# A hybrid decoder layer on one core: residual additions and the split of a late operand go in front of older ready work

## The chip, the core and the metric

The kernel runs on one NeuronCore of a Trainium2 chip. It uses five engines, each with its own instruction stream: TensorE (PE, matrix products, with a separate stream of weight loads, PEld), VectorE (DVE), ScalarE (ACT), GpSimd (POOL) and SyncE (SP, which here only issues transfers). The engines meet through semaphores, and each works through its own stream in order. The metric is the time of one execution on the device in microseconds (us): the median over repeated runs. One more execution was recorded by the hardware profiler; its trace is what is read below.

## What is computed

One decoder layer over 1024 tokens of width 1024: RWKV-7 time mixing and a sparse attention side by side, merged by gates, then a dense feed-forward block and a last normalisation. Cut to what the change touches:

```python
merged = g_a * (y_a @ w_o_rwkv) + g_b * (y_b @ w_o_att)
h = h + merged @ w_out
z = rmsnorm(h, norm2_g) @ w_ffn_in
z_gate, z_up = jnp.split(z, 2, axis=-1)
h = h + (jax.nn.silu(z_gate) * z_up) @ w_ffn_out
return rmsnorm(h, normf_g)
```

`y_a` comes from the RWKV recurrence over 64 x 64 states, `y_b` from the attention, in which each token attends to at most 256 keys that an indexer picked. The feed-forward width is 2816.

## The kernel before

**Tiles.** Activations lie with channels on the 128 partitions and tokens along the free dimension, in two halves of 512 tokens; the kernel calls them half 0 and half 1. Half 0 is the first half. A matrix of 1024 channels is eight slices of 128 x 512. Products are made to float32 accuracy from parts: `split` turns an operand into a rounded part on ACT (line 117) and a remainder on DVE (line 118), and a product is hi x hi, hi x lo and lo x hi (lines 143, 144 and 148, or 161 in `mm3_last`, or 1545, 1546 and 1548 in `joint`), 24 matmuls of 128 x 512 for 8 input slices. A weight slice comes by DMA into `wst` (three buffers, line 124) and is split into `whi` and `wlo` (two buffers each), at high priority. A product lands in one of three PSUM banks named `acc` or five named `mix`. Scratch `tmp` is a ring of four 128 x 512 buffers.

**Feed-forward.** The 22 slices of the feed-forward width go in three groups of 8, 8 and 6 (`GROUPS`). For the first two groups, `ffn_in` makes the gated slices and `ffn_out` multiplies them with the group's part of `w_ffn_out`: for each of eight output slices d it loads the running residual `d_h` from HBM into a `tmp` (line 1382), makes the product in an `acc` bank, adds the two on DVE (line 1388, the residual addition) and stores the result back (line 1392, on SP). With three banks, the product of slice d+3 cannot begin until the addition of slice d has read its bank. The last group of both halves is made together in `joint`, with the seven products of a Strassen-Winograd scheme: it first normalises half 1 (line 1575), loads half 0's operand again from `d_z` (line 1584, issued on POOL) and makes the combinations T1 and T2 (lines 1592, 1604 and 1610), and later T3 and T4 (lines 1592, 1633 and 1634), each split on ACT and DVE. `s_12271`, `s_12296`, `s_12554` and `s_12571` in the order below are T1 to T4, `s_12329` is B22.

**What runs beside what.** `fill` is a queue of generators; `pump` takes matmuls from it between the steps of the latency-bound stages. So half 0's `merge`, `ffn_in` and `ffn_out` of its first group stand between the steps of half 1's RWKV recurrence and its attention, and the output of half 0's middle group between half 1's `merge` and the start of `joint`. In the recurrence, each step goes S (line 885), products (850), `rhs` (860, four additions on DVE), products (869), `UV` (872 on ACT), products (881) and S again. Beside its last steps the selection of attention keys ends (lines 1053 to 1060), with scratch from the same `tmp` ring.

**The operand of half 0.** `normalise` makes half 0's feed-forward operand anew from `h` while the first slices of `ffn_in` run: four slices `za`, then four slices `zb` by way of `ts`, which are split last: the late split.

**What sets the order.** On PE the order is that of the program. On the other engines a scheduler chooses at build time among the instructions that it takes to be ready, and by default the older in program order goes first; what stands under `tc.high_priority()` goes in front. At run time every engine follows the order so chosen.

Of the kernel before, what the change touches and what calls it, by code (L numbers as in the profile page):

```python
# [19 lines left out]
ALU = mybir.AluOpType  # L20
# [30 lines left out]
def block_kernel(ctx: ExitStack, tc: tile.TileContext, ins: dict, outT: bass.AP, outR: bass.AP, stop=None, dbg=None):  # L51
    nc = tc.nc
    V, A, G, T, SY = nc.vector, nc.scalar, nc.gpsimd, nc.tensor, nc.sync
# [59 lines left out]
    def tmp():  # L113
        return tp.tile([128, HT], F32, tag="tmp", name="tmp")

    def split(hi, lo, x):
        A.activation(hi, x, AF.Copy)  # L117
        V.tensor_tensor(lo, x, hi.bitcast(F32), op=ALU.subtract)  # L118
# [8 lines left out]
    def weights(src, nk=8, rush=True, st=None, pool=None):  # L127
        with tc.high_priority() if rush else nullcontext():
            if st is None:
                st = raw_weights(src, nk)  # L130
            hi, lo = ((pool or wp).tile([128, nk, 128], F32R, tag=tag, name=tag, bufs=8 if pool else None)
                      for tag in ("whi", "wlo"))
            split(hi, lo, st)
        return hi, lo
# [3 lines left out]
    def mm3(ps, w, act, nk=8, wk=0, ak=0, tok=None):  # L138
        whi, wlo = w
        ahi, alo = act  # L140
        tok = slice(0, HT) if tok is None else tok
        for k in range(nk):
            T.matmul(ps, whi[:, wk + k, :], ahi[:, ak + k, tok], start=k == 0, stop=False)  # L143
            T.matmul(ps, whi[:, wk + k, :], alo[:, ak + k, tok], start=False, stop=False)  # L144
            if k % 2:
                yield 4
        for k in range(nk):
            T.matmul(ps, wlo[:, wk + k, :], ahi[:, ak + k, tok], start=False, stop=k == nk - 1)  # L148
            if k % 4 == 3 or k == nk - 1:
                yield k % 4 + 1  # L150

    def mm3_last(pss, ws, act, nk, tok=slice(0, HT), within=False):

        ahi, alo = act

        def terms(i, ks, js=range(3)):
            ps, (whi, wlo) = pss[i], ws[i]
            for j in js:
                w, a = ((whi, ahi), (wlo, ahi), (whi, alo))[j]
                for k in ks:  # L160
                    T.matmul(ps, w[:, k, :], a[:, k, tok], start=k == 0 and j == 0, stop=k == nk - 1 and j == 2)  # L161
                yield len(ks)

        n = len(pss) - within
        for i in range(n):
            yield from terms(i, range(nk - 1))
        if within:
            yield from terms(n, range(nk - 1), range(2))
        for i in range(n):
            yield from terms(i, range(nk - 1, nk))  # L170
        if within:
            yield from terms(n, range(nk - 1), (2,))
            yield from terms(n, range(nk - 1, nk))
# [17 lines left out]
    def but_last(gen):  # L191

        opened_tile[0] = True
        prev = next(gen)
        for n in gen:
            yield prev
            prev = n
        opened_tile[0] = False
        return prev
# [1091 lines left out]
    def parts(t):  # L1291
        return [t[:, k, :] for k in range(4)], [t[:, 4 + k, :] for k in range(4)]

    def normalise(zp, sq, row):

        h = sq.h

        def one(k, out):
            V.scalar_tensor_tensor(out, h[:, k, :], par[:, P_N2 + k:P_N2 + k + 1], row, op0=ALU.mult, op1=ALU.mult)
            SY.dma_start(d_z[k], out)  # L1300

        low, ts = zp.tile([128, 8, HT], F32R, tag="s2", name="za"), []
        for k in range(4):
            one(k, h[:, k, :])
            split(low[:, k, :], low[:, 4 + k, :], h[:, k, :])
        for k in range(4):
            ts.append(tmp() if k < 3 else tp.tile([128, HT], F32, tag="sacc", name="zt", bufs=2))
            one(4 + k, ts[k])
        high = zp.tile([128, 8, HT], F32R, tag="s0", name="zb")
        for k in range(4):  # L1310
            split(high[:, k, :], high[:, 4 + k, :], ts[k])
        return [Planes(*(a + b)) for a, b in zip(parts(low), parts(high))]

    def ffn_in(zp, tags, zs, gi, box):
# [4 lines left out]
        for j in range(gn):  # L1319
# [15 lines left out]
            if j < early:  # L1335
                x = tmp()
                V.tensor_tensor(x, pg, row, op=ALU.mult)
                A.activation(t, x, AF.Tanh, scale=0.5)
                V.scalar_tensor_tensor(t, t, 1.0, x, op0=ALU.add, op1=ALU.mult)
                V.scalar_tensor_tensor(x, pu, 0.5, row, op0=ALU.mult, op1=ALU.mult)  # L1340
                V.tensor_tensor(t, t, x, op=ALU.mult)
                if j == 0:
                    z = normalise(zp, sq, row)
                    opened_tile[0] = False
                    yield 4
                else:
                    zs[0] = z
            else:
                A.activation(t, pg, AF.Tanh, scale=0.5)
                V.scalar_tensor_tensor(t, t, 1.0, pg, op0=ALU.add, op1=ALU.mult)  # L1350
                V.scalar_tensor_tensor(t, pu, 0.5, t, op0=ALU.mult, op1=ALU.mult)
# [10 lines left out]
    def ffn_out(half, zp, f, gi, sqs=None):  # L1362
        gn = GROUPS[gi][1]
        final = sqs is not None
        if final:
            h = zp.tile([128, 8, HT], F32, tag="s2", name="h")
            sqs.append(Rms(h))
            for d in range(8):
                G.dma_start(h[:, d, :], d_h[half][d])

        def w(d):
            return weights(ins["w_fo1"][d] if final else ins["w_fo0"][gi, d], gn)

        bank = mix if final else acc
        pss = [bank() for _ in range(1 if final else 2)]
        last = yield from but_last(mm3_last(pss, [w(d) for d in range(len(pss))], f, gn, within=half == 1))
        for d in range(8):
            if final:
                t = h[:, d, :]
            else:  # L1380
                t = tmp()
                SY.dma_start(t, d_h[half][d])
            if d < len(pss):
                ps = pss[d]
            else:
                ps = bank()
                last = yield from but_last(mm3(ps, w(d), f, nk=gn))
            V.tensor_tensor(t, t, ps, op=ALU.add)  # L1388
            if final:
                sqs[0].add(d)  # L1390
            else:
                SY.dma_start(d_h[half][d], t)
            if d >= len(pss) - 1:
                yield last
# [99 lines left out]
    def ffn(half, zp, zs, tags):  # L1494

        for gi in range(JOINT):
            f = []
            yield from ffn_in(zp, tags, zs, gi, f)
            yield from ffn_out(half, zp, f[0], gi)
# [281 lines left out]
    credit[0] = 0  # L1781
    pump_whole(144 - 8)
    run_over(ffn_out(0, zp0, fj, JOINT, sq0))
    pump_whole(48)
    run_over(norm_out(0, sq0[0]))
# [90 lines left out]
```

## Time and profile before

| | us |
|---|---|
| median of three runs | 1756.36 (1756.19 to 1757.58) |
| profiled execution, its own time | 1753.59 |
| its span in the trace | 1751.7 |
| mean granted clock of TensorE | 0.988 of full speed |
| DVE busy in the span | 1127.6 (64%) |
| ACT busy | 869.6 (50%) |
| POOL busy | 133.8 (8%) |
| the 32 residual additions of line 1388 on `tmp` | 0.68 each, first at 924.2, last at 1709.0 |
| products of the first group's output, half 0 | from 904.74 to the next stage's first product at 977.18 |

A row of the order of time reads: start, duration, engine, line, operation, output<-inputs, shapes, count; at its end, in brackets, how long the engine sat idle before it and what released it. Starts are in us from the start of the span. Matmuls are pipelined, so a row's duration can reach over the next start; differences of starts are what counts.

### The profile page before, as it was taken

The page shows a single profiled execution, that of the slowest core. Times are in us where ns is not written, and L with a number is a line of the kernel's source. Part 1 is how long each engine was busy: PE and PEld are TensorE (multiplying, and loading weights), DVE is VectorE, ACT ScalarE, POOL GpSimd, SP SyncE. Part 2 cuts the span into 40 slices and gives each one's busy share as a digit, 9 for nine tenths or more (in the row PEclk, how much of TensorE's full clock was granted, in tenths as well). Part 3 has the DMA queues.
Part 4 walks back from the last instruction along what each step waited for, and adds up shares of the span by engine and source line. Part 5 has one row for each costly group of instructions (what it writes and reads, how often), then busy time and mean ns, then how long its engine had stood idle before and what let it go on. Part 6 is the DMA issues. An engine that isn't in the chain of part 4 may idle for free.

```text
span 1751.7 us, 26667 instructions
## 1 busy us (share of the span) xinstructions
PE 1694.3 (97%) x10000; PEld 1395.7 (80%) x10000; DVE 1127.6 (64%) x2206; ACT 869.6 (50%) x1685; POOL 133.8 (8%) x183
## 2 busy tenths in 40 slices
PE   8999999999999999999999999999979999999997
PEld 6888888888878777877787888888857788888887
DVE  6789899866577567858856544466577655433344
ACT  6365998554455788665334365533334333222322
POOL 0000000010022110001000311011000100000001
PEclk9999999999999999999999999999989999999999
DMA  5542334545376436734343764266622633553362
GB/s 209 178 139 87 107 91 141 174 108 160 109 214 169 146 102 197 225 112 137 90 121 100 228 172 127 91 226 203 187 83 90 193 112 108 172 168 102 115 214 80
DMA packets 144448, 253.44 MB, mean 145 GB/s; under 512 B 49680, under 2 KB 71888, under 8 KB 144192
## 3 DMA queue, kind: packets, MB, share of 16 engines
q1 hardware_dynamic: 115760, 161.84, 29.8%
q10 hardware_dynamic: 16128, 48.60, 8.8%
q0 software_dynamic: 12432, 41.30, 8.1%
q8 instruction: 79, 1.29, 0.3%
q14 instruction: 49, 0.40, 0.1%
HBM read 193.45 MB, written 58.25 MB: 144 GB/s over the span
## 4 chain that ended last, share of the span: by engine, by line
PE 41%; issue 6%; DVE 2%; DMA 1%; ACT 1%; POOL 1%; POOLq 0%; DVEq 0%; ACTq 0%
PE acc L148 9%; PE acc L143 9%; PE acc L144 9%; PE acc L161 3%; PE mix L1124 1%; PE mix L1100 1%; PE mix L1114 1%; PE mix L1548 1%; PE mix L1546 1%; PE mix L1545 1%; PE mix L148 1%; PE mix L144 1%; PE mix L143 1%; DMA wst<-in_w_ffn_in 0%; DMA d_h<-tmp 0%
## 5 line engine op out<-in xcount | busy, mean ns | idle before, releaser
L118 DVE TENSOR_TENSOR wlo<-wst,whi 128x1024 fp32r<-128x1024 f32 (+1 forms) x203 | 248.1, 1223 | 246.0 <-ACT whi L117 130.0
L117 ACT ACTIVATE whi<-wst 128x1024 fp32r<-128x1024 f32 (+1 forms) x203 | 212.6, 1049 | 278.4 <-PE acc L144 212.5
L143 PE MATMUL acc<-u1hi,whi 128*128 128x512 f32 x320 | 127.9, 400 | 0.0
L144 PE MATMUL acc<-u1lo,whi 128*128 128x512 f32 x320 | 125.1, 391 | 0.0
L143 PE MATMUL acc<-u0hi,whi 128*128 128x512 f32 (+1 forms) x320 | 122.8, 386 | 0.0
L144 PE MATMUL acc<-u0lo,whi 128*128 128x512 f32 (+1 forms) x320 | 121.3, 382 | 0.0
L143 PE MATMUL acc<-s,whi 128*128 128x512 f32 x256 | 99.8, 390 | 0.0
L144 PE MATMUL acc<-s,whi 128*128 128x512 f32 x256 | 99.6, 389 | 0.0
L143 PE MATMUL acc<-fhi,whi 128*128 128x512 f32 x192 | 76.9, 401 | 12.6 <-DVE tmp L1388 12.6
L148 PE MATMUL acc<-u1hi,wlo 128*128 128x512 f32 x320 | 81.8, 394 | 0.0
L148 PE MATMUL acc<-u0hi,wlo 128*128 128x512 f32 (+1 forms) x320 | 78.6, 384 | 0.0
L144 PE MATMUL acc<-flo,whi 128*128 128x512 f32 x192 | 76.0, 396 | 0.0
L1015 ACT ACTIVATE junkl<-kept,z 128x1024 int8<-128x1024 int16 (+1 forms) x64 | 69.4, 1084 | 4.7 <-DVE kept L984 4.4
L143 PEld LDWEIGHTS acc<-u1hi,whi 128*128 128x128 f32 x320 | 60.1, 188 | 12.6 <-issue 0.9
L1105 ACT ACTIVATE L<-L,mx 128x128 f32<-128x128 f32 (+7 forms) x64 | 49.5, 774 | 41.4 <-DVE mx L1102 40.8
L143 PEld LDWEIGHTS acc<-u0hi,whi 128*128 128x128 f32 x320 | 60.2, 188 | 11.9 <-issue 0.4
L144 PEld LDWEIGHTS acc<-u1lo,whi 128*128 128x128 f32 x320 | 60.2, 188 | 11.3
L144 PEld LDWEIGHTS acc<-u0lo,whi 128*128 128x128 f32 x320 | 60.2, 188 | 11.0
L148 PEld LDWEIGHTS acc<-u1hi,wlo 128*128 128x128 f32 x320 | 58.9, 188 | 12.5 <-issue 0.9
L148 PEld LDWEIGHTS acc<-u0hi,wlo 128*128 128x128 f32 x320 | 58.1, 188 | 11.9 <-issue 0.7
L148 PE MATMUL acc<-s,wlo 128*128 128x512 f32 x256 | 63.2, 389 | 0.0
L148 PEld LDWEIGHTS acc<-s,wlo 128*128 128x128 f32 x256 | 48.0, 188 | 10.0
(476 smaller groups left out, 4080.7 us busy)
## 6 DMA issues: line engine op xcount, KB each, us to landing
wst<-in_w_ffn_in SPq DMA_DIRECT2D x61, 512.0 KB
wst<-in_w_in ACTq DMA_DIRECT2D x36, 512.0 KB
wst<-in_w_in SPq DMA_DIRECT2D x27, 512.0 KB
wst<-in_w_fo SPq DMA_DIRECT2D x25, 512.0 KB
k<-d_k POOLq DMA_DIRECT2D x24, 512.0 KB, 8.0
d_g<-tmp ACTq DMA_DIRECT2D x32, 256.0 KB
wst<-in_w_ffn_in ACTq DMA_DIRECT2D x16, 512.0 KB
tmp<-d_h SPq DMA_DIRECT2D x32, 256.0 KB
```

The source lines that it names most:

```text
L117: A.activation(hi, x, AF.Copy)
L118: V.tensor_tensor(lo, x, hi.bitcast(F32), op=ALU.subtract)
L143: T.matmul(ps, whi[:, wk + k, :], ahi[:, ak + k, tok], start=k == 0, stop=False)
L144: T.matmul(ps, whi[:, wk + k, :], alo[:, ak + k, tok], start=False, stop=False)
L148: T.matmul(ps, wlo[:, wk + k, :], ahi[:, ak + k, tok], start=False, stop=k == nk - 1)
L161: T.matmul(ps, w[:, k, :], a[:, k, tok], start=k == 0 and j == 0, stop=k == nk - 1 and j == 2)
L1015: A.activation(junka[:, :n], y, AF.Sign, bias=z[:, i:i + 1], accum_out=cnt[:, i:i + 1])
L1100: T.matmul(ps[:, :w], q[bi // 2][:, e, bi % 2 * 128:bi % 2 * 128 + 128], k[:, i, e, c:c + w], start=i == 0, stop=i == 1)
L1105: A.activation(L[:, :n], L[:, :n], AF.Exp, scale=-1.0, bias=last, accum_out=sm[:, bi, e:e + 1])
L1114: T.transpose(ps[:, j * 128:(j + 1) * 128], L[:, (c + j) * 128:(c + j + 1) * 128], ident)
L1124: T.matmul(py[64 * e:64 * e + 64, bi * 128:(bi + 1) * 128], v[:, j, 64 * e:64 * e + 64], pts[e][j // 4][:, j % 4, :], start=j == b, stop=j ...
L1545: T.matmul(ps, whi[:, k, :], hi[k], start=opens and k == 0, stop=False, skip_group_check=True)
```

## The change

Two places change. In `normalise`, the four splits of the late slices are put under high priority. In `ffn_out`, the residual addition is put under high priority where it is not the last group's; loads, products, weight splits and the store keep theirs.

```diff
         high = zp.tile([128, 8, HT], F32R, tag="s0", name="zb")
-        for k in range(4):
-            split(high[:, k, :], high[:, 4 + k, :], ts[k])
+        with tc.high_priority():
+            for k in range(4):
+                split(high[:, k, :], high[:, 4 + k, :], ts[k])
         return [Planes(*(a + b)) for a, b in zip(parts(low), parts(high))]
...
-            V.tensor_tensor(t, t, ps, op=ALU.add)
+            with nullcontext() if final else tc.high_priority():
+                V.tensor_tensor(t, t, ps, op=ALU.add)
             if final:
                 sqs[0].add(d)
```

No instruction is added or removed, and PE's stream and POOL's stay as they were. After the change, lines behind 1309 have numbers higher by one and those behind 1387 by two (1388 becomes 1390, 1575 becomes 1577 and so on).

The first place is DVE's stream at the start of `joint`, where the output of half 0's middle group ends. Before, the piece behind the normalisation reads as follows; the addition of the first row is that of d=3, and `wlo` is the weight split of d=6, then of d=7.

```order
L1388 TENSOR_TENSOR tmp<-tmp,acc 128x512
L1575 SCALAR_TENSOR_TENSOR h<-h,par,row 128x512 x2
L1604 TENSOR_TENSOR t_12273<-h,t_12273 128x512
L1604 TENSOR_TENSOR t_12279<-h,t_12279 128x512
L1575 SCALAR_TENSOR_TENSOR h<-h,par,row 128x512
L118 TENSOR_TENSOR wlo<-wst,whi 128x1024
L118 TENSOR_TENSOR s_12271<-t_12273,s_12271 128x512
L118 TENSOR_TENSOR s_12271<-t_12279,s_12271 128x512
L1604 TENSOR_TENSOR t_12285<-h,t_12285 128x512
L1575 SCALAR_TENSOR_TENSOR h<-h,par,row 128x512 x2
L118 TENSOR_TENSOR s_12271<-t_12285,s_12271 128x512
```

Between this piece and the next stand 20 rows more, with the weight splits of d=7 and of the first product of `joint` among them. Then the additions of d=4, 5 and 6 follow, and after another weight split that of d=7:

```order
L1610 TENSOR_TENSOR t_12322<-t_12322,t_12324 128x512
L118 TENSOR_TENSOR s_12329<-h,s_12329 128x512
L1388 TENSOR_TENSOR tmp<-tmp,acc 128x512
L118 TENSOR_TENSOR s_12296<-t_12322,s_12296 128x512
L1388 TENSOR_TENSOR tmp<-tmp,acc 128x512 x2
L1523 TENSOR_TENSOR sr<-wst 128x512
L118 TENSOR_TENSOR sw<-sr,sw 128x512
L1528 TENSOR_TENSOR sr<-sr,wst 128x512
L118 TENSOR_TENSOR wlo<-wst,whi 128x1024
L1388 TENSOR_TENSOR tmp<-tmp,acc 128x512
```

After the change, the same stream from the addition of d=3:

```order
L1390 TENSOR_TENSOR tmp<-tmp,acc 128x512
L1577 SCALAR_TENSOR_TENSOR h<-h,par,row 128x512 x2
L1606 TENSOR_TENSOR t_12273<-h,t_12273 128x512
L1606 TENSOR_TENSOR t_12279<-h,t_12279 128x512
L1577 SCALAR_TENSOR_TENSOR h<-h,par,row 128x512
L1390 TENSOR_TENSOR tmp<-tmp,acc 128x512
L118 TENSOR_TENSOR wlo<-wst,whi 128x1024
L118 TENSOR_TENSOR s_12271<-t_12273,s_12271 128x512
L118 TENSOR_TENSOR s_12271<-t_12279,s_12271 128x512
L1606 TENSOR_TENSOR t_12285<-h,t_12285 128x512
L1577 SCALAR_TENSOR_TENSOR h<-h,par,row 128x512 x3
L1390 TENSOR_TENSOR tmp<-tmp,acc 128x512
```

The addition of d=4 stands ahead of the weight split of d=6, that of d=5 ahead of the weight split of d=7; those of d=6 and d=7 stand in the same way ahead of the next two weight splits.

The second place is DVE's stream in the last steps of half 1's recurrence, where the output of half 0's first group begins. Before, from the `rhs` of one step to the S of the next:

```order
L860 TENSOR_TENSOR rhs<-mix,rhs 64x2x64 x4
L1388 TENSOR_TENSOR tmp<-tmp,acc 128x512
L118 TENSOR_TENSOR wlo<-wst,whi 128x1024 x2
L1388 TENSOR_TENSOR tmp<-tmp,acc 128x512
L884 TENSOR_TENSOR S<-mix,S 128x256
L885 TENSOR_TENSOR S<-S,PC 128x256
L899 TENSOR_TENSOR yb<-mix,yb 128x512
L1056 TENSOR_SCALAR cnt<-cnt 128x1
L901 TENSOR_REDUCE mn<-yb 128x8
```

After the change the same piece:

```order
L860 TENSOR_TENSOR rhs<-mix,rhs 64x2x64 x3
L1390 TENSOR_TENSOR tmp<-tmp,acc 128x512 x2
L118 TENSOR_TENSOR wlo<-wst,whi 128x1024 x2
L860 TENSOR_TENSOR rhs<-mix,rhs 64x2x64
L884 TENSOR_TENSOR S<-mix,S 128x256
L1056 TENSOR_SCALAR cnt<-cnt 128x1
L885 TENSOR_TENSOR S<-S,PC 128x256
L899 TENSOR_TENSOR yb<-mix,yb 128x512
L901 TENSOR_REDUCE mn<-yb 128x8
```

Both additions and, with them, both weight splits now stand ahead of the fourth `rhs` addition. One step later (rows not shown here) the selection's lines 1054 and 1055 move ahead of the four `rhs` additions of that step, and each later addition ahead of the weight split next to it.

The third place is the late split on DVE. The rows are the same before and after; ACT's rows of `zb` are as well.

```order
L1299 SCALAR_TENSOR_TENSOR zt<-h,par,row 128x512
L118 TENSOR_TENSOR wlo<-wst,whi 128x1024
L118 TENSOR_TENSOR zb<-tmp,zb 128x512 x3
L604 TENSOR_SCALAR x_8281<-x_8281 128x1024
L631 TENSOR_SCALAR x_8323<-x_8282,hb 128x256
L606 SCALAR_TENSOR_TENSOR x_8281<-rmask,x_8281 128x256
L118 TENSOR_TENSOR zb<-zt,zb 128x512
```

Nothing moved there.

## The prediction

> **What bounds the kernel now.** I read the page first, then the waits of TensorE (PE), then the order of time around the longest of them.
>
> ```profile
> PE 1694.3 (97%) x10000; PEld 1395.7 (80%) x10000; DVE 1127.6 (64%) x2206; ACT 869.6 (50%) x1685; POOL 133.8 (8%) x183
> ```
>
> TensorE is busy for 1694.3 of 1751.7 us. Its program order is written out by hand, so whatever it waits for delays everything behind. The change can win only out of the 57.4 us in which PE is idle, and out of the stretches after a wait in which its clock is lower.
>
> ```profile
> PE acc L143 <- DVE tmp L1388: 12.6, 1, 12.6
> ...
> PE acc L143 <- ACT zb L117: 3.3, 1, 3.3
> PE mix L869 <- DVE rhs L860: 3.2, 2, 2.6
> ```
>
> This is the view of who waited for whom (total, times, longest). The longest wait of the whole run is a single one: a product that needs an `acc` bank waits for a residual addition (L1388). The second row belongs to the late split (`zb`), the third to the end of the RWKV stage, where the other set of moved additions stands. Those three places are the case.
>
> ```profile
> 1259.36 0.39 PE L143 MATMUL acc<-fhi,whi 128*128 128x512 f32 x1
> ...
> 1262.99 1.98 PE L148 MATMUL acc<-fhi,wlo 128*128 128x512 f32 x8
> ...
> 1282.97 0.77 PE L143 MATMUL acc<-fhi,whi 128*128 128x512 f32 x1 [12.57 <-DVE tmp L1388]
> ...
> 1288.03 1.98 PE L148 MATMUL acc<-fhi,wlo 128*128 128x512 f32 x8
> ```
>
> In the order of time on PE (start, duration), slice d=5 of the middle group starts at 1259.36, so d=4 was finished then and its addition could run. Slice d=7 needs the bank of d=4 and waits 12.57 us. Its first 16 products then take 1288.03 - 1282.97 = 5.06 us, where those of d=5 took 1262.99 - 1259.36 = 3.63: 1.43 us more, at a lowered clock (the granted clock stands third from the end in the rows of stretches below).
>
> ```profile
> 1259.06 0.74 DVE L1575 SCALAR_TENSOR_TENSOR h<-h,par,row 128x512 f32<-128x512 f32 x1
> ...
> 1282.15 0.68 DVE L1388 TENSOR_TENSOR tmp<-tmp,acc 128x512 f32<-128x512 f32 x1
> ```
>
> VectorE (DVE) held that addition back from 1259.80 to 1282.15, behind normalisations, combinations and splits of `joint` that were ready.
>
> **The change, part by part.** No instruction is added or removed.
>
> *The joint start, the main term.* The addition of d=4 now stands right behind the instruction of 1259.06, so it ends near 1260.4. Slice d=7 can begin when d=6 ends, at 1282.97 - 12.57 = 1270.40; the bank is free 10 us before. The wait of 12.57 and the 1.43 at the lowered clock go: 14.0 us on PE.
>
> What is late next? VectorE must do the same work in less time:
>
> ```profile
> 1256.50:1321.10 64.60, 50.14 (x77) 0.92 0.31 101
> 1255.00:1285.00 30.00, 25.65 (x40) 0.84 0.46 143
> 1285.00:1303.00 18.00, 7.18 (x11) 0.98 0.11 42
> 1303.00:1321.00 18.00, 17.27 (x30) 1.00 0.29 87
> ```
>
> These are VectorE's busy times by stretch (stretch, length, busy time, granted clock of PE, share of the DMA engines, GB/s). Between the row factor's arrival (1256.5) and the last split of the fourth combination (T4), it is busy 50.14 of 64.60 us. The room is 14.46 us, most of it in 1285 to 1303, where it waited for PE. Without PE's gap it needs 50.14 us in 64.60 - 14.0 = 50.6. And T4 was already a wait:
>
> ```profile
> 1321.13 0.50 PE L1546 MATMUL mix<-s,sw 128*128 128x512 f32 x1 [0.31 <-DVE s L118]
> ```
>
> So PE gains what VectorE gains: 14.46 less the idle that stays. What stays are waits for others:
>
> ```profile
> 1266.36 0.69 DVE L1604 TENSOR_TENSOR t<-h,t 128x512 f32<-128x512 f32 x1 [1.69 <-DMA t<-d_z]
> ...
> 1278.53 0.69 DVE L1610 TENSOR_TENSOR t<-t,t 128x512 f32<-128x512 f32 x1 [1.20 <-DMA t<-d_z]
> ```
>
> These two make 2.89 us; the loads are issued when a split releases a buffer, and the additions (0.68 each) that now stand among these instructions fill a part. At worst all idle of the first and third stretch stays, 4.35 + 0.73 = 5.08: a gain of 9.4. At best 0.46 stays: 14.0. I take two thirds of the two rows, 1.9, and so **12.5**.
>
> SP issues the store of each addition in order, and in the new order the stores of d=4, 5 and 6 stand between the loads of the next weights, where all four stood behind them:
>
> ```profile
> 1260.97 13.11 SPq L124 DMA_DIRECT2D wst<-in_w_ffn_in  x3
> 1282.86 9.43 SPq L1392 DMA_DIRECT2D d_h<-tmp  x4
> ```
>
> A load waits for the weight split that frees its buffer, which now follows an addition: 0.68 us plus an issue of some 0.3. The last of the three was issued by 1274.08, and its first reader stands in VectorE's order behind the additions of 1282.15, so it had 8 us; I cost this at nothing, and should that slack be gone, at 1 us a load. On PE all else is in place: the splits for T1 and T2 and the first weights precede their products in the new order.
>
> *The end of RWKV.* The same edit moves the first group's additions, and this part may lose.
>
> ```profile
> 922.93 1.25 DVE L860 TENSOR_TENSOR rhs<-mix,rhs 64x128 f32<-64x128 f32 x4 [1.26 <-PE mix L850]
> 924.21 0.69 DVE L1388 TENSOR_TENSOR tmp<-tmp,acc 128x512 f32<-128x512 f32 x1
> 924.82 2.35 DVE L118 TENSOR_TENSOR wlo<-wst,whi 128x1024 fp32r<-128x1024 f32 x2
> ```
>
> Now the fourth of the four `rhs` additions stands behind two residual additions and both weight splits. Three `rhs` end at 922.93 + 0.94 = 923.87; two additions (0.61 from start to start), the splits (2.35) and 0.31 bring the fourth to 927.7 instead of 924.2. The products that need it:
>
> ```profile
> 924.22 0.68 PE L869 MATMUL mix<-rhs,TT 64*64 64x64 f32 x16
> ```
>
> PE is through with the first three quarters at 924.7: a **new wait of 3.0 us**, on the recurrence, so all behind it is late.
>
> What goes is the wait that stood a step later, the larger of the two that make the 3.2 us of the third row above:
>
> ```profile
> 936.81 1.01 PE L869 MATMUL mix<-rhs,TT 64*64 64x64 f32 x6 [2.58 <-DVE rhs L860]
> ```
> ```profile
> 933.48 1.15 ACT L1053 ACTIVATE tmp<-kept,ge 128x1024 bf16<-128x1024 f32 x1 [4.96 <-DMA d_h<-tmp]
> ```
>
> VectorE stood behind a selection count (L1056) that waited for this ScalarE instruction, and that for the store of d=1 to free a scratch buffer. The addition of d=1 moves from 924.82 + 2.35 = 927.2 to 924.5 and its store with it, 2.7 us earlier, and the 3.2 us go. So does the slow clock behind them:
>
> ```profile
> 938.00:940.00 2.00, 1.51 (x12) 1.30 (x13) 0.48 (x3) 1.74 (x6) 1.35 (x1) 0.50 0.00 0
> 940.00:942.00 2.00, 2.00 (x16) 1.25 (x16) 1.21 (x2) 0.21 (x1) 0.29 (x1) 0.50 0.00 0
> 942.00:944.00 2.00, 2.00 (x14) 1.59 (x11) 1.97 (x4) 0.00 (x0) 0.00 (x0) 0.50 0.18 16
> ```
>
> The granted clock is 0.50 for 5.51 us of PE work, which costs 2.76. Together 6.0 us go. The new wait of 3.0 may lower the clock too, by nothing to 2.76; I take half, 1.4.
>
> Then comes a second new wait. Before, the third step's `rhs` additions came first, and two selection instructions behind them:
>
> ```profile
> 948.33 1.25 DVE L860 TENSOR_TENSOR rhs<-mix,rhs 64x128 f32<-64x128 f32 x4 [4.23 <-PE mix L850]
> 949.62 0.75 DVE L1054 TENSOR_SCALAR tmp<-kept,top 128x1024 bf16<-128x1024 f32 x1
> 950.40 2.29 DVE L1055 TENSOR_TENSOR_SCAN kept<-tmp 128x1024 f32<-128x1024 bf16 x1
> ```
>
> Now both (3.04 us) stand in front of `rhs`, and the first needs a buffer that the store of d=2 frees.
>
> ```profile
> 942.63 0.68 DVE L1388 TENSOR_TENSOR tmp<-tmp,acc 128x512 f32<-128x512 f32 x1
> ```
> ```profile
> DMA to landing us min/median/max: 2.8/4.3/5.3
> ```
>
> That addition (first row) now stands ahead of its weight split and ends about 1.2 us earlier, near 942.1. A transfer of this tensor lands 2.8 to 5.3 us after its issue (second row, the view of the tensor `d_h`), so `rhs` starts at 947.9 to 950.4 against 948.33: -0.4 to +2.1, and I take 0.9, the middle. The sum of what is added is 3.0 + 1.4 + 0.9 = 5.3 against 6.0 removed, with bounds of 2.6 and of 10.6 (a second lowered clock of 2.76 at the upper one). I take **0**, between a gain of 3.4 and a loss of 4.6, since the two sums are as near as the bounds are wide.
>
> [...]
>
> *The late split.* Its four rows stand at the same places in the new order on both engines that run it, so the 3.3 us of the second row above stay: **0**. A loss has no way in either, with the order unchanged.
>
> *The remaining additions* (middle group d=0 to 3, second half) stand ahead of a weight split instead of behind it:
>
> ```profile
> 1552.92 1.23 DVE L118 TENSOR_TENSOR wlo<-wst,whi 128x1024 fp32r<-128x1024 f32 x1 [3.62 <-ACT whi L117]
> ```
>
> Addition and split wait for the same product to end, VectorE idles 3.62 us ahead of each such pair (this row is of the second half, in the tail), and the split's product is a slice away: **0**, hidden by that slack; without it, 0.68 us (the addition) for each of some 20.
>
> *Sum:* 12.5 + 0 + 0 + 0. The profiled execution took 1753.59 us (the span and 1.89 around it) and becomes 1741.1; the median, 1756.36, lies 2.77 above and becomes **1743.9**.
>
> **Rivals.**
>
> *VectorE falls behind at the joint start:* all 5.08 us of idle stay, 9.4 us are won: 1747.0, and with the loss of 4.6 at RWKV 1751.6. For it: 50.14 us in 50.6 leaves nothing for a late transfer. Against: two of the additions stand just ahead of instructions that waited for transfers. Chance 0.14.
>
> *The gap only changes its name:* something else, the first weights or T2, holds PE as long, and the time stays at 1756.4. For it: only the last waiter is shown. Against: in the order of before, the weight splits of d=7 and of the first product of `joint` stand ahead of the addition of d=4, so they were done when PE went on. Chance 0.05.
>
> *Slower:* at the end of RWKV every step of the recurrence meets a wait of some 3 us and the clock stays at half. Each us at half costs 0.5; against 12.5 + 6.0 - 0 it decides from 37 us at half. If it stayed so to the end of the first group's products, 49 us later, 24.5 - 18.5 = 6 us lost: 1762.4. For it: a wait of 2.58 us brought 6 us of half clock. Against: only two steps are left after the first new wait. Chance 0.04.
>
> *The change does not do what it says:* for the split this is so, and it is in the forecast.
>
> **How the numbers follow.** The forecast, 0.77, spans 1756.36 - 14.0 - 2 = 1740.4 to the first rival. The range goes from 1740.4 to 1750.4, a gain of 9.4 less 3.4 of RWKV loss; the outer cases hold the rest. About 0.2% (3.5 us) is what a measurement of this kernel can tell from no change, so faster means under 1752.8: 0.77 + 0.14, less 0.01 for the first rival's edge, 0.90. Same is 0.05 + 0.01, slower 0.04.
>
> **What would show it.** Right: the wait of 12.57 on the addition is gone from PE's waits, with the row of `zb` unchanged; VectorE is busy almost without a break from the row factor to T4; waits at T4 are longer than 0.31 us; a wait of about 3 us of L869 on L860 stands near 925. Wrong: a wait over 5 us of PE on weights or T2 between slice d=7 and T4, or PE's clock at half for over 10 us after 925.

## The result, and the profile after

| | before | after |
|---|---|---|
| median of four runs of each | 1756.28 us (1755.78 to 1757.58) | 1738.62 us (1737.26 to 1742.58) |
| ratio | | 0.9904, 95% interval 0.9888 to 0.9919 |
| profiled execution: its time, span | 1753.59, 1751.7 us | 1737.26, 1735.0 us |
| granted clock of TensorE, mean | 0.988 | 0.993 |

The change makes the kernel 17.7 us faster (14.2 to 19.7). The forecast was 12.5 us: right in sign and in place, too small in size, and the time lies 1.8 us under the range. The page's line of the engines after:

```profile
PE 1690.0 (97%) x10000; PEld 1392.3 (80%) x10000; DVE 1126.0 (65%) x2206; ACT 869.6 (50%) x1685; POOL 134.1 (8%) x183
```

The instructions are the same. Of the 16.7 us by which the span is shorter, 4.3 are PE's busy time (a higher mean clock) and 12.4 were idle time. What PE waits for now (view of the waits: total, times, longest):

```profile
PE acc L143 <- ACT zb L117: 3.3, 1, 3.3
PE mix L869 <- DVE rhs L860: 3.1, 1, 3.1
```

The row with 12.6 us is gone. The late split has its 3.3 as before, and the wait for `rhs` is another one of about the same size.

**The joint start.** PE in order of time, after (start, duration), the same four places as in the prediction: d=5 begins, its last eight products, d=7 begins, its last eight.

```profile
1257.64 0.39 PE L143 MATMUL acc<-fhi,whi 128*128 128x512 f32 x1
...
1261.27 1.98 PE L148 MATMUL acc<-fhi,wlo 128*128 128x512 f32 x8
...
1268.52 0.39 PE L143 MATMUL acc<-fhi,whi 128*128 128x512 f32 x1
...
1272.15 1.98 PE L148 MATMUL acc<-fhi,wlo 128*128 128x512 f32 x8
```

From d=5 to the end of d=7's first 16 products it takes 1272.15 - 1257.64 = 14.51 us, where it took 1288.03 - 1259.36 = 28.67. So 14.16 us are won here: the whole wait and the whole lowered clock, without a deduction. Nothing of it is given back up to T4. The PE waits at T4, before and then after:

```profile
1318.64 0.49 PE L1546 MATMUL mix<-s,sw 128*128 128x512 f32 x1 [0.30 <-DVE s L118]
1320.32 0.49 PE L1545 MATMUL mix<-s,sw 128*128 128x512 f32 x1 [1.19 <-ACT s L117]
1321.13 0.50 PE L1546 MATMUL mix<-s,sw 128*128 128x512 f32 x1 [0.31 <-DVE s L118]
```
```profile
1302.74 0.50 PE L1548 MATMUL mix<-s,sw 128*128 128x512 f32 x1 [0.29 <-DVE s L118]
1304.43 0.50 PE L1547 MATMUL mix<-s,sw 128*128 128x512 f32 x1 [1.18 <-ACT s L117]
1305.23 0.50 PE L1548 MATMUL mix<-s,sw 128*128 128x512 f32 x1 [0.31 <-DVE s L118]
```

They are the same three waits to a hundredth, although VectorE has lost nearly all of its slack in between. (In `residual_only`, below, which has the same order on every engine, the first of them is 0.54, and PE loses 0.25 us there.) Its stretch from the row factor to T4 after (length, then busy time of PE, PEld, DVE, ACT and POOL, granted clock, DMA share, GB/s), and four rows of VectorE in it:

```profile
1254.81:1305.18 50.37, 48.65 (x213) 39.46 (x211) 49.61 (x77) 24.03 (x38) 4.98 (x9) 1.00 0.40 129
```
```profile
1258.01 0.68 DVE L1390 TENSOR_TENSOR tmp<-tmp,acc 128x512 f32<-128x512 f32 x1
...
1265.87 0.68 DVE L1606 TENSOR_TENSOR t<-h,t 128x512 f32<-128x512 f32 x1
...
1280.23 0.69 DVE L1612 TENSOR_TENSOR t<-t,t 128x512 f32<-128x512 f32 x1 [0.45 <-DVE s L118]
...
1285.10 0.69 DVE L1561 TENSOR_TENSOR tmp<-tmp,mix 128x512 f32<-128x512 f32 x1
```

The addition of d=4 runs at 1258.01, ten us before d=7 needs its bank. The stretch shrank from 64.60 to 50.37 us, and VectorE is busy in 49.61 of them: 0.76 us of idle is left, of 14.46. The two instructions that had waited 1.69 and 1.20 us for loads of `d_z` (1604 and 1610 before, 1606 and 1612 now) no longer wait for one. The last row is the second eviction of a product of `joint`; before, it read

```profile
1300.98 0.69 DVE L1559 TENSOR_TENSOR tmp<-tmp,mix 128x512 f32<-128x512 f32 x1 [3.02 <-issue]
```

VectorE sat idle 3.02 us ahead of it. The view names no releaser, but the last matmul of that product starts at 1300.50 and takes 0.39 us, so the product was not ready before. The row now starts 15.88 us earlier, and PE's products in front of it also start 15.88 us earlier (1288.03 to 1272.15). The product is ready at 1285.00 and VectorE comes free at 1285.07: it reaches that row just in time.

**The end of RWKV.** VectorE, then PE, after:

```profile
921.56 0.93 DVE L860 TENSOR_TENSOR rhs<-mix,rhs 64x128 f32<-64x128 f32 x3 [1.26 <-PE mix L850]
922.41 1.26 DVE L1390 TENSOR_TENSOR tmp<-tmp,acc 128x512 f32<-128x512 f32 x2
923.60 2.34 DVE L118 TENSOR_TENSOR wlo<-wst,whi 128x1024 fp32r<-128x1024 f32 x2
925.98 0.29 DVE L860 TENSOR_TENSOR rhs<-mix,rhs 64x128 f32<-64x128 f32 x1
```
```profile
926.32 0.90 PE L869 MATMUL mix<-rhs,TT 64*64 64x64 f32 x10 [3.06 <-DVE rhs L860]
...
938.09 0.99 PE L869 MATMUL mix<-rhs,TT 64*64 64x64 f32 x16
```

The fourth `rhs` addition stands behind two additions and two weight splits, and PE waits 3.06 us for it. The clock behind that wait (stretch, length, PE busy, granted clock, DMA share, GB/s):

```profile
926.00:928.00 2.00, 1.68 (x12) 0.50 0.69 262
928.00:930.00 2.00, 2.00 (x6) 0.50 0.98 369
930.00:932.00 2.00, 2.00 (x6) 0.50 0.02 8
932.00:934.00 2.00, 2.00 (x52) 0.97 0.04 8
```

That is 5.7 us of PE work at half clock, which costs 2.85. One step later (938.09) PE no longer waits; before, it waited 2.58 and 0.66 there, also with a lowered clock behind. Over the stage the two nearly cancel: the same product of PE starts 1.38 us earlier than before ahead of it (923.66 before) and 2.23 us earlier behind it (1003 us), a gain of 0.85.

### The profile page after: what moved, and what is told of

Read it like the earlier page. It is cut to its first block, busy times and chain, and to the rows that moved or that the text cites. A ratio compares the mean times of both kernels' runs of the same rounds, so it can differ in the third digit from the quotient of the medians.

```text
span 1735.0 us, 26657 instructions
## 1 busy us (share of the span) xinstructions
PE 1690.0 (97%) x10000; PEld 1392.3 (80%) x10000; DVE 1126.0 (65%) x2206; ACT 869.6 (50%) x1685; POOL 134.1 (8%) x183
## 4 chain that ended last, share of the span: by engine, by line
PE 43%; issue 6%; DVE 2%; POOL 1%; ACT 1%; DMA 1%; POOLq 0%; DVEq 0%; ACTq 0%
PE acc L148 9%; PE acc L143 9%; PE acc L144 9%; PE acc L161 3%; PE mix L1124 1%; PE mix L1100 1%; PE mix L1114 1%; PE mix L1550 1%; PE mix L1548 1%; PE mix L1547 1%; PE mix L148 1%; PE mix L144 1%; PE mix L143 1%; DMA wst<-in_w_ffn_in 0%; PE acc L1548 0%
## 5 line engine op out<-in xcount | busy, mean ns | idle before, releaser
L143 PEld LDWEIGHTS acc<-u1hi,whi 128*128 128x128 f32 x320 | 60.1, 188 | 12.6 <-issue 0.9
L148 PEld LDWEIGHTS acc<-u1hi,wlo 128*128 128x128 f32 x320 | 58.9, 188 | 12.5 <-issue 0.9
L1390 DVE TENSOR_TENSOR tmp<-tmp,acc 128x512 f32<-128x512 f32 x32 | 21.8, 683 | 54.1 <-PE acc L148 39.6
```

## The experiments

The ratios are to the kernel before on the same chip; the stages are compared by the starts of the same PE products in the profiled executions. In the code of an experiment the change's two places have the line numbers of after.

### Which additions carry the gain

Three runs put one group of additions in front each and leave the late split as before. The condition is `half == 0 and gi == 1` for `mid_only`, `half == 0 and gi == 0` for `first_only`, `half == 1 and not final` for `half1_only`. A fourth, `residual_only`, has all of them. Of the later runs only `split_early` has the late split's priority.

```diff
-            V.tensor_tensor(t, t, ps, op=ALU.add)
+            with tc.high_priority() if half == 0 and gi == 1 else nullcontext():
+                V.tensor_tensor(t, t, ps, op=ALU.add)
```

> Only the eight residual additions of half 0's middle group go in front; those of the first group and of half 1, and the late split, stay as before. Theory A, the bank alone: the 12.57 us wait on the acc bank and the 1.43 us at the lowered clock both go whole and VectorE keeps up, 14.0 us, so about 1742.3 us. Theory B, the forecast's term: VectorE has no room and 1.9 us of its idle time stay, 12.5 us, so about 1743.8 us. Theory C, the gain comes as much from the other additions: 1747 us or more.

> Only the eight additions of half 0's first group, at the end of the RWKV stage, go in front. Theory A, from the trace of the change: the new wait of 3.06 us with its half clock and the old wait of 2.58 us with its own nearly cancel, a gain of about 1 us: 1755.3 us. Theory B, the forecast: 0, with bounds of 1752.9 and 1760.9 us. The acc wait of 12.6 us at the joint start stays in both.

> Only the additions of half 1 go in front. Theory A: their slack hides them, 0: 1756.3 us. Theory B: the 0.8 us by which the trace of the change runs ahead of before near 1390 us, and the rest of the time that joint and RWKV do not account for, come from here: about 1754.7 us.

> All residual additions go in front, the late split stays as before; the order on every engine is that of the whole change. Theory A, the split does nothing: the time of the whole change, 1738.6 us within 1. Theory B, the split's priority does count: some 3 us more, 1742.

| run | median, us | ratio, 95% interval |
|---|---|---|
| before | 1754.91 | |
| `mid_only` | 1741.37 | 0.9926 (0.9906 to 0.9945) |
| `first_only` | 1754.73 | 0.9996 (0.9980 to 1.0012) |
| `half1_only` | 1755.61 | 1.0001 (0.9989 to 1.0012) |
| `residual_only` | 1740.20 | 0.9918 (0.9900 to 0.9936) |

The middle group carries it: a gain of 13.0 us (9.7 to 16.5). These times alone can't tell theory A (14.0) from B (12.5). The trace can: in `mid_only` PE gains 14.2 us from d=5 to the last products of d=7, and its waits at T4 are as before. In `first_only` the new wait of 3.0 us stands, that of 2.58 is gone, and PE gains 0.8 us over the stage, within the timing's interval of 0.7 us gained (3.5 gained to 2.1 lost). Half 1's additions bring nothing, neither in the time nor, near 1390 us, in the trace. All additions without the split give the time of the whole change within the intervals, and the order of its trace is the same, row by row, on all engines, so the split's priority does nothing.

### One addition

`d4_only` has the same edit with the condition `half == 0 and gi == 1 and d == 4`.

> Of all residual additions only one goes in front, that of slice d=4 of half 0's middle group; the other 31 and the late split stay as before. Theory A, one bank held by one addition: this alone brings the 12.57 us of wait and the 1.43 us at the lowered clock, 14.0 us, against before. Theory B, the banks of d=5 to 7 are late next: part of the wait comes back at a later product on an acc bank, and the gain is under 10 us.

1743.48 us against 1757.17, ratio 0.9918 (0.9903 to 0.9933): theory A, for a gain under 10 us lies outside the interval. PE in order of time, the last products of d=6 and then the two places of d=7:

```profile
1272.50 1.98 PE L148 MATMUL acc<-fhi,wlo 128*128 128x512 f32 x8
1274.31 0.39 PE L143 MATMUL acc<-fhi,whi 128*128 128x512 f32 x1
...
1277.94 1.98 PE L148 MATMUL acc<-fhi,wlo 128*128 128x512 f32 x8
```

No wait, full clock (1.00), 14.2 us won, with the priority of a single instruction of 0.68 us raised. (The scheduler then also places other rows of VectorE and ScalarE near it in another order.) The additions of d=5 to 7 still run 6 to 15 us later than in the change, against the products around them, and PE does not wait for their banks. In this run one load of `d_z` is still waited for, by 0.30 us, so the two waits of 2.89 us shrink without the other three additions: what fills them is other ready work that the new order places there.

### Has VectorE room?

The forecast made VectorE the bound at the joint start and took 1.9 us off. Three runs change its load there, all with every residual addition in front. `dve_plus4` and `dve_plus12` add one and three instructions behind each of the additions of d=4 to 7 (a number n of 1 or 3); `dve_minus3` leaves three additions out.

```diff
                 V.tensor_tensor(t, t, ps, op=ALU.add)
+                if half == 0 and gi == 1 and d >= 4:
+                    for _ in range(n):
+                        V.tensor_tensor(t, t, t, op=ALU.max)
```
```diff
-                V.tensor_tensor(t, t, ps, op=ALU.add)
+                half == 0 and gi == 1 and d > 4 or V.tensor_tensor(t, t, ps, op=ALU.add)
```

> All residual additions in front, and behind each of the additions of d=4 to 7 of half 0's middle group one more VectorE instruction of the same size (the maximum of the sum with itself, which changes nothing), 4 x 0.61 us = 2.4 us of VectorE's time more at the start of the joint stage. Theory A, VectorE is the bound there and has only the 0.66 us of its idle time left: PE waits 1.8 us more by the end of T4, against the run with all additions in front. Theory B, VectorE still has room that its busy time does not show: under 0.5 us more.

> As the run with one more instruction behind each of four additions, but with three: 12 x 0.61 = 7.3 us of VectorE's time more. Theory A: 7.3 - 0.66 = 6.7 us more of waits on PE by the end of T4. Theory B: under 3 us more.

> All residual additions in front, but the additions of d=5, 6 and 7 of half 0's middle group are left out (the residual keeps its old value for these three slices), 3 x 0.61 = 1.8 us of VectorE's time less at the start of the joint stage; the scheduler then draws some rows there closer together. Theory A, VectorE is the bound there: what PE waits for at T4, 1.8 us in the run with all additions in front, goes whole or nearly, and PE ends the stage up to 1.8 us earlier. Theory B, that wait comes from the chain of T4 itself, which begins when PE gives something free, and not from VectorE's load: the wait stays within 0.3 us.

| run | ratio, 95% interval | second eviction on VectorE: late against PE | lost by PE by the end of T4 |
|---|---|---|---|
| `residual_only` | 0.9918 (0.9900 to 0.9936) | 0.1 us | 0.25 us |
| `dve_plus4` | 0.9922 (0.9908 to 0.9937) | 1.2 us | 4.9 us |
| `dve_plus12` | 0.9958 (0.9943 to 0.9972) | 4.6 us | 6.4 us |
| `dve_minus3` | 0.9893 (0.9872 to 0.9913) | 0 | 0 |

The third column is how much less that row has moved forward than PE's last products of d=7. In `dve_plus4` the second eviction (L1564 there) reads

```profile
1290.10 0.68 DVE L1564 TENSOR_TENSOR tmp<-tmp,mix 128x512 f32<-128x512 f32 x1
```

10.88 us earlier than before, where PE's products start 12.10 earlier (1288.03 to 1275.93). At T4 PE then waits

```profile
1309.92 0.77 PE L1550 MATMUL mix<-s,sw 128*128 128x512 f32 x1 [4.81 <-DVE tmp L1675]
```

in one piece, in place of the three waits that add up to 1.8, and the clock falls behind it:

```profile
1308.00:1312.00 4.00, 2.08 (x5) 0.54 0.10 20
1312.00:1316.00 4.00, 4.00 (x12) 0.61 0.85 281
```

So in this execution 2.4 us more on VectorE cost 4.9 on PE, more than theory A said: 3.0 in the longer wait, the rest in the clock. (The times, with their intervals of 3 us to each side, don't resolve it, here or in `dve_minus3`, and the new order also draws a few other rows there differently.) Twelve instructions, 7.3 us, cost 6.4 by the end of T4, close to A's 6.7, though only 4.4 of it are longer waits and the rest is the clock (0.57 of full speed over the 4 us from 1312); another wait of 1.7 us on a weight split follows right behind. Upwards there is no room: theory A. Downwards theory B holds. In `dve_minus3` the waits at T4 stay (PE, order of time), and VectorE waits for PE again:

```profile
1312.16 0.50 PE L1548 MATMUL mix<-s,sw 128*128 128x512 f32 x1 [0.20 <-DVE s L118]
1313.84 0.51 PE L1547 MATMUL mix<-s,sw 128*128 128x512 f32 x1 [1.18 <-ACT s L117]
1314.65 0.50 PE L1548 MATMUL mix<-s,sw 128*128 128x512 f32 x1 [0.30 <-DVE s L118]
```
```profile
1294.60 0.69 DVE L1561 TENSOR_TENSOR tmp<-tmp,mix 128x512 f32<-128x512 f32 x1 [0.27 <-PE mix L1550]
```

The reading that fits all three is that the 1.8 us at T4 belong to a chain that begins when PE hands over that second product (eviction, then T3 and T4 in VectorE's order) and ends some 20 us of VectorE's time later. As long as VectorE is back at the eviction in time, PE keeps everything or nearly; in the change it is back with nothing to spare.

### The price at the end of RWKV

`rhs_first` leaves the first addition of the first group (d=0) at the priority of before; all others go in front.

```diff
-            with nullcontext() if final else tc.high_priority():
+            with tc.high_priority() if not final and not (half == 0 and gi == 0 and d < 1) else nullcontext():
                 V.tensor_tensor(t, t, ps, op=ALU.add)
```

> As the run with all residual additions in front, but for the first addition (d=0) of half 0's first group, which keeps the priority of before: on VectorE all four rhs additions then stand ahead of the additions of d=0 and d=1, and these ahead of the weight splits. Theory A, the new wait of 3.06 us and its half clock (some 3 us) were the price of the change at the end of RWKV and the old wait of 2.58 us does not come back: 6 us faster than all additions in front, 20 us faster than before. Theory B, the old wait comes back, since the selection count stands ahead of the next rhs: no gain beyond 1 us on all additions in front.

1734.05 us against 1757.17, ratio 0.9864 (0.9850 to 0.9879): 23.9 us, the fastest ratio so far, its interval clear of that of the change. VectorE, ScalarE and PE in order of time:

```profile
924.43 1.25 DVE L860 TENSOR_TENSOR rhs<-mix,rhs 64x128 f32<-64x128 f32 x4 [1.26 <-PE mix L850]
925.71 1.28 DVE L1390 TENSOR_TENSOR tmp<-tmp,acc 128x512 f32<-128x512 f32 x2
926.91 2.35 DVE L118 TENSOR_TENSOR wlo<-wst,whi 128x1024 fp32r<-128x1024 f32 x2
```
```profile
929.68 1.15 ACT L1053 ACTIVATE tmp<-kept,ge 128x1024 bf16<-128x1024 f32 x1 [0.74 <-DVE wlo L118]
```
```profile
925.69 0.68 PE L869 MATMUL mix<-rhs,TT 64*64 64x64 f32 x16
...
934.95 1.08 PE L869 MATMUL mix<-rhs,TT 64*64 64x64 f32 x16
```

Neither wait is left. All four `rhs` come first, and the addition of d=1 still goes ahead of the weight splits. ScalarE's instruction that had sat 4.96 us for a store of the residual now waits 0.74 us, and not for a store. PE gains 7.0 us over the stage, 6.1 more than in the change. Theory A, and a version that beats both kernels.

### The late split, moved for good

On ScalarE the four `zb` stand behind the rounding of `nr` (128 x 16), which waits for GpSimd. After the change, ScalarE in order of time:

```profile
820.15 0.21 ACT L117 ACTIVATE nr<-nr 128x16 fp32r<-128x16 f32 x1 [3.57 <-POOL nr L652]
```

The first `zb` follows at 820.39.

`split_early` is the whole change with that rounding on GpSimd, `rhs_first_split_early` is `rhs_first` with it.

```diff
+    psplit = lambda hi, lo, x: (G.tensor_copy(hi, x), V.tensor_tensor(lo, x, hi.bitcast(F32), op=ALU.subtract))
...
-            split(nr2[:, :, 0, :].bitcast(F32R), nr2[:, :, 1, :].bitcast(F32R), nr3)
+            (psplit if q == 3 else split)(nr2[:, :, 0, :].bitcast(F32R), nr2[:, :, 1, :].bitcast(F32R), nr3)
```

> The whole change, and in the last quarter of each half's RWKV preparation the rounded part of nr (128 x 16) is made on GpSimd, right behind the power it comes from, where ScalarE made it. On ScalarE the late split (zb) then no longer stands behind an instruction that waits 3.57 us for GpSimd; no other instruction of ScalarE or VectorE moves. Theory A, what held the late split is that in-order wait and not its priority: PE's waits on zb (3.34 + 0.23 + 0.89 = 4.5 us) go, and with them the lowered clock behind them (0.61 and 0.54 of full speed over 8 us, some 3 us): 4.5 to 7.5 us faster than the whole change. Theory B, the split is late by its own data or PE then waits for nr as long: under 1 us.

> The run with the first addition of the first group at the priority of before, and nr's rounded part on GpSimd as well. If the two gains stand in different stages they add: some 6 us from the one and 4.5 to 7.5 us from the other, 11 to 13 us faster than the whole change, near 1728 us. If the second only moves a wait into the recurrence, 1734 us as without it.

1737.63 and 1731.71 us against 1754.07, ratios 0.9905 (0.9885 to 0.9926) and 0.9861 (0.9840 to 0.9883). By the times alone the split's part can't be told from nothing. In the trace of `split_early` it can, in ScalarE and PE:

```profile
816.95 0.64 ACT L117 ACTIVATE fhi<-tmp 128x512 fp32r<-128x512 f32 x1 [0.99 <-PE acc L148]
817.49 1.14 ACT L117 ACTIVATE zb<-tmp 128x512 fp32r<-128x512 f32 x2
```
```profile
822.33 0.50 PE L144 MATMUL acc<-zb,whi 128*128 128x512 f32 x1 [1.38 <-DVE zb L118]
825.73 0.50 PE L143 MATMUL acc<-za,whi 128*128 128x512 f32 x1 [1.06 <-DVE tmp L1338]
```

ScalarE goes straight on to `zb`. Of PE's waits 2.4 us are left in place of 4.5, now on the fourth split on VectorE, which stands behind three other instructions, and on an instruction that reads the previous bank; against before, PE's products start 0.14 us later ahead of this place and 3.65 earlier behind it. That is 3.8 us won here, and the same 3.8 in `rhs_first_split_early`; `residual_only` wins nothing here, and the change lost 0.8 in its profiled execution. It is more than theory B and, against `residual_only`, less than A's 4.5 to 7.5, so the mechanism holds and a part of the wait came back behind it. Why the times don't show it stays open in part: of the 3.8 us, the profiled execution of `split_early` lost 1.4 again at T4, where the clock fell behind the same three waits. The two gains together were expected to bring 11 to 13 us over the change; in the traces they bring 3.8 + 6.1 = 9.9 in their two places, and by the ratios some 7.5.

## Why the prediction was right in place and too small in size

| step of the prediction | forecast | measured |
|---|---|---|
| joint start: PE's wait and lowered clock | 14.0 won | 14.16 won |
| **VectorE's idle that stays comes off that** | 1.9 lost | **0** (0.76 stays) |
| RWKV: new wait on the fourth `rhs` | 3.0 lost | 3.06 |
| its lowered clock | 1.4 lost | 2.85 |
| second new wait, on lines 1054 and 1055 | 0.9 lost | 0 |
| what goes there | 6.0 won | gone as forecast |
| RWKV, taken as | 0 | 0.85 won |
| late split; half 1's additions | 0; 0 | 0; 0 |
| middle group's additions d=0 to 3 | 0 | 0.55 lost |

**The step that failed** is the deduction at the joint start: "PE gains what VectorE gains: 14.46 less the idle that stays", with 1.9 us taken for what stays. Of VectorE's idle 0.76 us stayed, its busy time came out 0.53 shorter (50.14 to 49.61), and so its stretch shrank by 14.23 us, as much as PE gained. The size was wrong, and the reading behind it too: the waits at T4 were taken as a sign that VectorE is the bound. They were 1.8 us before and in the change, and 1.7 in `dve_minus3`, where VectorE has 1.8 us of work less. VectorE was no bound but a limit that PE came up to and did not pass. Its idle was not all one pool, either: it had to be back at the second eviction on time, and the idle time that it spent waiting for PE there counts as room in full. Of the prediction's signs, the wait that is gone, the row of `zb`, the busy VectorE and the new wait near 925 all came; longer waits at T4 did not. `dve_plus4` shows how near it was: the rival in which VectorE falls behind needs 2.4 us more work at most.

**The two `d_z` waits** were costed as if their loads were fixed and only the moved additions could fill them. 0.45 us of idle is left at one of the two places and that is for a split, and `d4_only` shows 0.30 with one addition moved. Other ready work filled them.

**RWKV** had the right mechanism for what goes and for the first new wait, which is off by 0.06 us. The lowered clock was taken at the middle of its bounds and came at the upper one, 2.85 against 2.76, and the second new wait did not come. VectorE's row of line 1054 after:

```profile
943.68 0.75 DVE L1054 TENSOR_SCALAR tmp<-kept,top 128x1024 bf16<-128x1024 f32 x1
```

It begins without a pause, 2.0 us after the addition of d=2 ended (941.65). It does need the buffer that this addition's store frees, as forecast, but the store was quick. The 2.8 to 5.3 us of the forecast were not those of stores: the view could time 16 transfers of the tensor, all of them loads on GpSimd's queue. The store of d=2 on SP, before and then after:

```profile
942.74 0.34 SPq L124 DMA_DIRECT2D wst<-in_w_fo  x1
943.33 0.32 SPq L1392 DMA_DIRECT2D d_h<-tmp  x1
```
```profile
941.68 0.32 SPq L1394 DMA_DIRECT2D d_h<-tmp  x1
942.82 0.34 SPq L124 DMA_DIRECT2D wst<-in_w_fo  x1
```

Before, it went out 0.59 us behind a weight load; now it goes out 1.14 us ahead of one, since the addition stands ahead of the weight split that lets the load go. By the trace's semaphore records, which the views don't print, the store landed at 947.61 before, 4.28 us after its issue, and at 943.65 after the change, 1.97 us after its issue and 0.03 ahead of line 1054. The errors partly cancel: the clock cost 1.45 more, the second wait 0.9 less. So 5.9 was added against 6.0 removed, and the 0.85 won are mostly small things that the forecast did not list, such as a wait of 0.33 for `UV` near 928 that is gone. That they came out near its 0 is in part luck. Behind 3.06 us of waiting the granted clock fell to 0.50, as it had behind 2.58 us before.

**The remaining additions** were put at nothing, hidden by VectorE's slack, and that was wrong in one place. In the middle group the addition of d=1 now stands ahead of two weight splits and three splits of `ylo`, an operand of half 1's `merge`. VectorE before, then after:

```profile
1158.06 0.68 DVE L1388 TENSOR_TENSOR tmp<-tmp,acc 128x512 f32<-128x512 f32 x1
```
```profile
1151.74 0.68 DVE L1390 TENSOR_TENSOR tmp<-tmp,acc 128x512 f32<-128x512 f32 x1
```

The three splits end 0.6 us later against the products around them, and three matmuls that read `ylo` now start right behind the split that they need. PE loses 0.55 us there. The same loss stands in the traces of all nine kernels that have the middle group's additions in front, and of none of the three others.

**The rest of the 17.7 us.** Between the two profiled executions the span differs by 16.7 us. The stages that the change touches make 14.5 of it: 14.16 at the joint start and 0.85 at RWKV, less 0.55 for the remaining additions. The other 2.2 belong to these two executions. 0.8 is further on in `joint`, 0.5 of it in shorter waits; it comes in `mid_only` and `d4_only` too, but not in `residual_only`, whose order is that of the change. And 1.3 is a dip of the clock in unchanged code, which the last section shows. The missing 1 us to the difference of the medians lies within their spread. `residual_only` gives 14.4 us (11.2 to 17.5), and a true gain of 14.5 us fits both intervals. So the failed step is worth 1.7 of the 5.3 us by which the time came out under the forecast, RWKV 0.85, and most of what lies beyond is chance between executions.

## What to carry to other kernels

A long wait on a buffer may hang on one short instruction that stands late in an in-order stream: here 12.57 us hung on an addition of 0.68 us, and moving that one was enough. Moving its kind everywhere bought a new wait of 3.06 us where it passed the four `rhs` of a recurrence. When a faster engine meets one that is almost busy, ask at which row the second must be back for the first, not how busy it is over the stretch: up to that row 0 to 0.25 us was lost here, beyond it 4.9 us for 2.4 of added work and 6.4 for 7.3. Ask too what the moved instruction lets go first: here the store of d=2 that went out 1.14 us ahead of a weight load landed in 1.97 us, and in 4.28 us where it went out 0.59 us behind one. A raised priority changed nothing for the `zb` splits, whose rounding stood on ScalarE behind a wait of 3.57 us for GpSimd, so compare the order first.

## What the runs showed of the hardware that was not expected

**The clock dips in code that no one touched.** The same stretch of RWKV, before and after (granted clock third from the end):

```profile
846.00:852.00 6.00, 5.43 (x61) 0.76 0.20 56
```
```profile
846.00:852.00 6.00, 5.43 (x73) 1.00 0.29 64
```

1.4 us are lost in the one and none in the other, with the same code and the same wait ahead (3.43 us, in both). It is the change's execution that is the exception: the products that took 5.98 us here before took 4.88 in it, and 5.65 to 6.18 in the profiled executions of the eleven experiments. At T4 it goes the other way: behind waits of 0.36, 1.18 and 0.19 us the clock fell in `split_early` and cost 1.4 us (the next four products took 1.91 us), and behind 0.29, 1.18 and 0.31 it did not in the change (1.09 us for the same four). Near 743 us products slow down in the same way behind waits for `TZ` that some executions have and some don't: in `dve_minus3` behind 0.52, 0.25 and 0.15 us they start 0.43 us apart, not 0.23, and from the first product on `TZ` to the next step's first on `rhs` it is 10.88 us, where it was 7.54 before, without such waits. A good part of the spread of the kernel before, 1751.6 to 1766.7 us in 23 runs, can lie there; how much was not measured.

**A store behind a weight load took twice as long.** In the two traces, 18 stores of the residual have no transfer but other such stores issued in the 4 us ahead of them, and they land 1.96 to 2.02 us after their issue. The 12 that go out 0.6 to 0.7 us behind a weight load, with nothing else but such stores in those 4 us, take 4.0 to 4.4 us; nine of the 18 have a weight load 1.1 to 1.2 us behind them and land in 1.96 to 2.01 us. The change turns that order round for most stores, and the median of all 32 falls from 4.2 to 2.3 us. What slows them was not shown.

**A GpSimd instruction became longer.** The power on `nr` (L652) took 4.41 us in the change, where VectorE stood idle beside it for 2.8 us of that time, and 6.82 us in both runs (`split_early` and `rhs_first_split_early`) in which VectorE made the `zb` splits at the same time. Spans on GpSimd are rough, but the two agree. What made it longer was not shown.
